# One kernel, seven edits: half-width first projections, normalising on GpSimd, a later top-k selection, a different split of expert passes, and five shared PSUM banks

## The chip, the cores and the metric

The kernel runs on one core of one Trainium2 chip. The metric is the time of one execution on the device, in microseconds (us). The core has five engines that run their own instruction lists in order and wait for each other by semaphores: TensorE (PE, its weight loads shown apart as PEld), VectorE (DVE), ScalarE (ACT), GpSimd (POOL) and SyncE (SP), which here only issues transfers. Transfers (DMA) run on queues beside the engines.

## The reference

512 tokens of width 1024 go through three layers in float32 and a last norm. Cut to what matters:

```python
# layer 1
h = rms_norm(x);  u, q, k, v, f, g1, g2 = split(h @ w_in)
x += (sigmoid(g1) * s5_branch(u) + sigmoid(g2) * forgetting_attention(q, k, v, f)) @ w_out   # 8 heads of 128
x += peer_ffn(rms_norm(x), w_query, sub_keys, peer_u, peer_v)     # 16384 experts, 8 heads x top 16
# layer 2: "even"
y = rmsnorm(x) @ ev_w_in
o_a = dsa_mixer(...)        # 8 latent heads; an indexer scores all tokens and keeps the top 128 of each row
o_b = diff_mixer(...)       # 4 differential heads: softmax_0 - lambda * softmax_1
x += concat(o_a, o_b) @ ev_w_out;   x += swiglu(rmsnorm(x))
# layer 3: "odd"
y = rmsnorm(x) @ od_w_in
o = nsa_mixer(...)          # 16 heads in 4 groups: compressed, selected and window branches, gated
x += o @ od_w_out;   x += swiglu(rmsnorm(x))
out = rmsnorm(x)
```

## The kernel before

All activations stay on the chip as four tiles of 128 tokens. A float32 product is made of three fp32r matmuls (mm3, lines 331 to 334): each operand is split into a high and a low part, and high x high, high x low and low x high are added in PSUM. Weights come in units of 128 x 1024 through Stream (lines 64 to 82): SP issues the load (L67), ACT copies the high part (L75), and DVE subtracts it for the low part (L81), or, for keys that stand in ADDED, ACT writes the negated high part (L78) and a transfer on POOL's queue adds the raw weights to it (L79). Three units are kept ahead of PE.

The program is written as Python generators and a scheduler orders each engine's list from its own estimate of when each instruction can run; nothing is reordered on the chip. Work that is to fill holes (the selection, output projections) is put in a list bg, and each call of yield_bg(n) takes n steps of it at that place in the program; drain_bg takes what is left.

- norm_T (L310 to L329) norms one token tile after another on DVE (xn, L323), transposes it on PE (L326) and splits it on ACT and DVE (hhi L275, hlo L276). A projection with proj_T (L336) multiplies a weight unit with all 512 tokens at once, so its first matmul needs all four tiles. proj_256 (L370) goes tile by tile, but unit by unit outside that.
- Layer 1's expert layer streams peer_u and peer_v, one unit of 512 KB for each of 128 expert blocks, for three of the four token tiles; the rows of the remaining tile's experts are gathered by POOL (L979) and used by DVE (L988, L996). Of the 128 u passes N_SPILL = 72 go before the v passes, with their results written to memory (at) and read back (a4); the last N_LATE = 8 of these come after the last of the gates. The other 56 stand between v passes.
- The even mixer runs the indexer, then 4 differential heads through pipeline, which computes a head's scores (diff_first, L1508) before the head ahead of it is finished (diff_second, L1534: transposes, products, a sum of squares, rsqrt on DVE, on = L1555, and the transposes of on that PE waits for). selection (L1487) is the background of these heads: 16 rounds of MAX8 (L1493) and MATCH_REPLACE8 (L1494) on three rows of tiles, 96 instructions on DVE in 48 steps and a last step that makes masks of them (L1497). It has to be whole before the 8 latent heads. The differential half of the output projection (out_parts, L1599: four column blocks of three steps) is then the background of the latent heads.
- The odd mixer runs 32 items (16 heads x 2 branches) through pipeline: first (L1856) makes four blocks of scores with 128, 256, 384 and 512 keys, each in a PSUM bank of its own from a pair named sx, masks and reduces them on DVE (L1868) and exponentiates on ACT (L1870); second (L1874) scales the four blocks (DVE L1882 for r = 0 and 2, ACT L1880 for r = 1 and 3), transposes them into banks from a set of three named tx (L1887), splits on ACT and DVE, and multiplies with the values (L1897, L1898).
- normalise (L1321) does the same scaling for layer 1's heads and the latent heads: r = 0, 1, 2 on DVE (L1329), r = 3 on ACT.

## Time and profile before

| | |
|---|---|
| median of 3 runs | 3279.72 us (3277.26 to 3280.32) |
| profiled execution | 3279.84 us, of which the span in the trace is 3278.1 us |
| mean granted TensorE clock | 0.978 |
| busy: PE, DVE, ACT, POOL | 95%, 64%, 46%, 22% of the span |

The profile is of one execution. A time at the left of a row counts from the start of the span. A row of a timeline or of a group ends with the idle time of that engine just before, and what ended it. PE clock 1.00 means 2.4 GHz and 0.50 means 1.2 GHz; a stretch's figure is the mean over it.

### The profile page before, as it was taken

The numbers are of one execution on the slowest core, as the hardware profiler recorded it, in microseconds if no ns is written. First come the engines' busy times: TensorE is split into PE (matmuls) and PEld (weight loads), VectorE is DVE, ScalarE is ACT, GpSimd is POOL, SyncE is SP. The second block draws the span as 40 slices with busy tenths as digits, with TensorE's granted clock in tenths as the row PEclk, the third lists the DMA queues.
The fourth block names the chain that finished last, engine by engine and source line by source line (L and its number), as shares of the span: only waits on it lengthen the run. The fifth ranks groups of instructions, "written<-read, shape, count | busy, mean of one in ns | idle before, by whom it ended". The sixth has DMA issues, their size and how long they took to land.

```text
span 3278.1 us, 46646 instructions
## 1 busy us (share of the span) xinstructions
PE 3128.9 (95%) x17107; PEld 2742.3 (84%) x17107; DVE 2108.7 (64%) x4643; ACT 1519.0 (46%) x2966; POOL 709.5 (22%) x873
## 2 busy tenths in 40 slices
PE   7999999999989999999999986999999998999999
PEld 6998878999988878999998975878888986778887
DVE  6786349999757778887885686643324388743323
ACT  4555233559963333333335664632222378732222
POOL 1561000020015554666662310000000110000000
PEclk9999999999999999999999997999999999999999
DMA  6553232476779998999997641122233210123332
GB/s 177 142 136 115 97 116 84 153 247 243 258 271 342 340 342 300 343 336 324 345 335 205 146 107 42 43 90 97 96 97 124 84 46 10 49 73 98 98 92 83
DMA packets 232758, 551.28 MB, mean 168 GB/s; under 512 B 19785, under 2 KB 113865, under 8 KB 230609
## 3 DMA queue, kind: packets, MB, share of 16 engines
q1 hardware_dynamic: 184432, 349.58, 32.1%
q0 software_dynamic: 43776, 159.40, 15.6%
q10 hardware_dynamic: 4320, 39.32, 3.1%
q8 instruction: 134, 2.20, 0.3%
q14 instruction: 96, 0.78, 0.1%
HBM read 472.60 MB, written 49.82 MB: 159 GB/s over the span
## 4 chain that ended last, share of the span: by engine, by line
PE 81%; DVE 10%; ACT 3%; DMA 3%; issue 2%; POOL 0%; SPq 0%; DVEq 0%; POOLq 0%; ACTq 0%
PE mm L332 21%; PE mm L333 21%; PE mm L334 21%; PE ax L334 2%; PE ax L332 2%; PE ax L333 2%; PE ax L1137 2%; DMA wraw<-in_peer_v_dram 1%; DVE wlo L81 1%; PE tx L1317 1%; PE tx L1887 1%; PE po L1897 1%; DVE xn L323 1%; DVE tl L276 1%; ACT whi L75 1%
## 5 line engine op out<-in xcount | busy, mean ns | idle before, releaser
L75 ACT CAST whi<-wraw 128x1024 fp32r<-128x1024 f32 x525 | 549.2, 1048 | 880.1 <-PE mm L333 325.2
L81 DVE TENSOR_TENSOR wlo<-wraw,whi 128x1024 fp32r<-128x1024 f32 x477 | 600.2, 1258 | 544.0 <-ACT whi L75 537.1
L334 PE MATMUL mm<-hhi,wlo 128*128 128x512 f32 (+1 forms) x1544 | 577.8, 374 | 2.6 <-DVE wlo L81 2.6
L332 PE MATMUL mm<-hhi,whi 128*128 128x512 f32 (+1 forms) x1544 | 577.3, 375 | 0.0
L333 PE MATMUL mm<-hlo,whi 128*128 128x512 f32 (+1 forms) x1544 | 577.2, 374 | 0.0
L332 PE MATMUL mm<-whi,hhi 128*128 128x256 f32 (+1 forms) x1280 | 382.1, 300 | 8.1 <-ACT hhi L275 3.9
L333 PE MATMUL mm<-wlo,hhi 128*128 128x256 f32 (+1 forms) x1280 | 382.4, 299 | 2.0 <-DMA wlo<-wraw 2.0
L334 PE MATMUL mm<-whi,hlo 128*128 128x256 f32 (+1 forms) x1280 | 380.3, 299 | 0.0
L334 PEld LDWEIGHTS mm<-hhi,wlo 128*128 128x128 f32 x1544 | 290.1, 188 | 43.3 <-DVE wlo L81 3.2
L332 PEld LDWEIGHTS mm<-hhi,whi 128*128 128x128 f32 x1544 | 290.4, 188 | 41.4 <-ACT hhi L275 0.7
L333 PEld LDWEIGHTS mm<-hlo,whi 128*128 128x128 f32 x1544 | 290.1, 188 | 40.7 <-DVE hlo L276 0.2
L333 PE MATMUL mm<-wlo,wth 128*128 128x512 f32 x768 | 303.5, 395 | 0.1
L334 PE MATMUL mm<-whi,wtl 128*128 128x512 f32 x768 | 302.5, 394 | 0.0
L979 POOL DMA_INDIRECT rw<-in_peer_rows_dram,idx x128 | 159.9, 1249 | 562.4 <-DVE act L988 339.5
L332 PE MATMUL mm<-whi,wth 128*128 128x512 f32 x768 | 257.6, 397 | 9.4 <-ACT whi L75 9.3
L332 PEld LDWEIGHTS mm<-whi,hhi 128*128 128x128 f32 x1280 | 248.4, 194 | 15.6 <-ACT hhi L275 4.1
L333 PEld LDWEIGHTS mm<-wlo,hhi 128*128 128x128 f32 x1280 | 248.3, 194 | 8.9 <-DMA wlo<-wraw 2.2
L334 PEld LDWEIGHTS mm<-whi,hlo 128*128 128x128 f32 x1280 | 247.2, 194 | 5.9
L1203 ACT CAST wth<-w 128x384 fp32r<-128x384 f32 x128 | 65.7, 514 | 354.9 <-POOL w L1200 209.7
L979 POOL DMA_INDIRECT rw<-in_peer_v_dram,idx x128 | 184.8, 1444 | 113.9 <-DVE acc L996 84.0
L988 DVE CUSTOM_DVE_ANT_0 rw<-rw,hrow 128x1024 f32<-128x1024 f32 x128 | 179.5, 1411 | 9.5 <-DMA rw<-in_peer_rows_dram,idx 9.5
L996 DVE SCALAR_TENSOR_TENSOR acc<-rw,act,acc 128x1024 f32<-128x1024 f32 x127 | 173.8, 1369 | 12.7 <-DMA rw<-in_peer_v_dram,idx 12.0
(567 smaller groups left out, 6111.5 us busy)
## 6 DMA issues: line engine op xcount, KB each, us to landing
wraw<-in_peer_u_dram SPq DMA_DIRECT2D x128, 512.0 KB
wraw<-in_peer_v_dram SPq DMA_DIRECT2D x128, 512.0 KB
wlo<-wraw POOLq DMA_DIRECT2D x48, 512.0 KB
gt<-gst ACTq DMA_DIRECT2D x12, 2048.0 KB
g<-gt SPq DMA_DIRECT2D x32, 768.0 KB
wraw<-in_w_gate_dram SPq DMA_DIRECT2D x44, 512.0 KB
wraw<-in_w_up_dram SPq DMA_DIRECT2D x44, 512.0 KB
wraw<-in_w_down_dram SPq DMA_DIRECT2D x44, 512.0 KB
```

The costliest lines, as they stand in the source:

```text
L75: self.nc.scalar.copy(hi[:, :w], r[:, :w])
L81: self.last = self.nc.vector.tensor_sub(lo[:, :w], r[:, :w], hi[:, :w])
L276: V.tensor_sub(lo, ps, hi)
L323: V.scalar_tensor_tensor(xn, x[:, o], rs, grow[:, o], op0=ALU.mult, op1=ALU.mult)
L332: PE.matmul(ps, ah, bh, start=start, stop=False)
L333: PE.matmul(ps, ah, bl, start=False, stop=False)
L334: PE.matmul(ps, al, bh, start=False, stop=stop)
L979: G.indirect_dma_start(out=rw, out_offset=None, in_=A[("peer_rows", "peer_v")[m]], in_offset=bass.IndirectOffsetOnAxis(ap=idx[:, k:k + 1], ...
L988: V.tensor_tensor_reduce(rw, rw, hrow, 1.0, 0.0, op0=ALU.mult, op1=ALU.add, accum_out=act[:, k:k + 1])
L996: V.scalar_tensor_tensor(acc0, rw, act[:, k:k + 1], acc0, op0=ALU.mult, op1=ALU.add)
L1137: PE.matmul(ps[:, i * P:(i + 1) * P], o2[:, i], og[:, i], start=True, stop=True)
L1203: S.copy(wh, w)
```

## The change

1. **Late passes.** N_SPILL goes from 72 to 76, N_LATE from 8 to 12 and DOTS_C from 28 to 32: twelve u passes, not eight, stand between the last gates and the first v pass, and four fewer between v passes.
2. **Halves.** The first three units of w_u, of w_query and of both SwiGLUs (gate 0, up 0, gate 1) are multiplied with the first 256 tokens and then with the last 256 (proj_T_first). These twelve units and the odd mixer's first two become ADDED. The first projections of the even and odd mixer go token tile by token tile over both of their units (by_tile).
3. **GpSimd normalising.** normalise puts r = 0 and 1 on POOL, r = 2 on DVE, r = 3 on ACT, and the odd mixer's second now calls it.
4. **Later selection.** The background steps at the differential heads' projections go from 2 to 1 and between their stages from 3 to 1. Nothing is drained after the heads; three steps are taken after each of four query projections, and three after each of the first six steps of out_parts, which now come before the latent heads.
5. The latent heads' weights (uk, uv) are loaded on POOL's queue, not SP's.
6. The odd mixer's norm gain is loaded ahead of the first SwiGLU.
7. **Shared banks.** The odd mixer has five banks tx for scores and transposes; the scores of r = 0 and 1 share one; all scores of an item are issued ahead of DVE's reading; transposes come as j = 2, then 1 and 3 in one bank, then 0.

```diff
@@ -28,13 +28,15 @@
 NE = 128
-N_SPILL = 72
-DOTS_C = 28
-N_LATE = 8
+N_SPILL = 76
+DOTS_C = 32
+N_LATE = 12
...
-ADDED = ("w_kq", "w_v", "ev_a", "ev_iq", "ev_qk", "ev_vb", "ev_qn")
+ADDED = ["w_kq", "w_v", "ev_a", "ev_iq", "ev_qk", "ev_vb", "ev_qn"]
+ADDED += [(n, m) for n in ("u", "w_query") for m in range(3)] + [("od_kv", 0, kk) for kk in range(2)]
+ADDED += [k for i in range(2) for k in (("gate", i, 0), ("up", i, 0), ("gate", i, 1))]
@@ -73,7 +75,7 @@
         self.nc.scalar.copy(hi[:, :w], r[:, :w])
-        if self.specs[i][0][0] in ADDED:
+        if self.specs[i][0] in ADDED or self.specs[i][0][0] in ADDED:
@@ -338,6 +340,19 @@
+    def proj_T_first(keys, h):
+        us = [ws.get(k, 2 - i) for i, k in enumerate(keys)]
+        pss = [bank_m() for _ in us]
+        for f in range(2):
+            c = slice(256 * f, 256 * f + 256)
+            for ps, (wh, wl) in zip(pss, us):
+                for k in range(KD):
+                    w = slice(k * P, k * P + P)
+                    mm3(ps[:, c], wh[:, w], wl[:, w], h[0][:, k, c], h[1][:, k, c],
+                        k == 0 and f == 0, k == KD - 1 and f == 1)
+        return pss
@@ -367,10 +382,19 @@
-    def proj_256(key, h, c0, nk=KD, tick=2, k0=0):
+    def proj_256(key, h, c0, nk=KD, tick=2, k0=0, by_tile=False):
 
         pss = [bank_m() for _ in range(2)]
-        for kk in range(k0 // 4, nk // 4):
+        if by_tile:
+            us = [ws.get((key, c0, kk), 1) for kk in range(2)]
+        for q in range(NT if by_tile else 0):
+            o = pss[q // 2][:, 256 * (q % 2):256 * (q % 2) + 256]
+            for k in range(KD):
+                wh, wl = us[k // 4]
+                c = slice(k % 4 * 256, k % 4 * 256 + 256)
+                mm3(o, h[0][:, k, q * P:(q + 1) * P], h[1][:, k, q * P:(q + 1) * P], wh[:, c], wl[:, c],
+                    k == 0 and q % 2 == 0, k == KD - 1 and q % 2 == 1)
+        for kk in range(k0 // 4, 0 if by_tile else nk // 4):
@@ -421,6 +445,10 @@
         if 4 + 2 * layer in phases:
+            if layer == 0 and 5 in phases:
+                state["gain"] = ExitStack()
+                state["grow"] = load_gain(A["norm_mix"][1:2], state["gain"].enter_context(
+                    pool_in(tc, name="gain", bufs=1)))
@@ -532,6 +560,7 @@
         V.tensor_sub(wfl, wf, wfh)
+        psu = K["proj_T_first"]([("u", m) for m in range(3)], h)
@@ -826,7 +855,7 @@
         for m in range(4):
-            ps = proj_T(("u", m), h)
+            ps = psu[m] if m < 3 else proj_T(("u", m), h)
@@ -1026,8 +1055,9 @@
                 SY.dma_start(keys, A["sub_keys"])
+                psq = K["proj_T_first"]([("w_query", m) for m in range(3)], h)
                 for m in range(16):
-                    ps = proj_T(("w_query", m), h)
+                    ps = psq[m] if m < 3 else proj_T(("w_query", m), h)
@@ -1266,11 +1296,12 @@
         al = fp.tile([P, NF, T], F32R, name="al")
+        first = K["proj_T_first"]([("gate", i, 0), ("up", i, 0), ("gate", i, 1)], h)
         for m in range(NF):
-            pg = proj_T(("gate", i, m), h)
+            pg = first.pop(0) if first else proj_T(("gate", i, m), h)
             sg = fp.tile([P, T], F32, tag="sg", bufs=3, name=nm("sg"))
             S.activation(sg, pg, AF.Silu)
-            pu = proj_T(("up", i, m), h)
+            pu = first.pop(0) if first else proj_T(("up", i, m), h)
@@ -1323,7 +1354,9 @@
         W = P * (r + 1)
-        if r == NT - 1:
+        if r < 2:
+            nc.gpsimd.tensor_scalar(Ps[r][:, :W], Ps[r][:, :W], fac[:, r:r + 1], None, op0=ALU.mult)
+        elif r == NT - 1:
@@ -1414,7 +1447,7 @@
         qr = ep.tile([P, NT, 8, 32], F32, name="qr")
-        pss = proj_256("ev_a", h, 0)
+        pss = proj_256("ev_a", h, 0, by_tile=True)
@@ -1557,7 +1590,7 @@
             for hd in range(4):
-                pss = proj_256("ev_qk", h, 256 * hd)
+                pss = proj_256("ev_qk", h, 256 * hd, tick=1)
@@ -1575,17 +1608,18 @@
                 if hd < 2:
-                    pss = proj_256("ev_vb", h, 256 * hd)
+                    pss = proj_256("ev_vb", h, 256 * hd, tick=1)
...
-        pipeline(K, diff_heads(), lambda: yield_bg(3))
-        drain_bg()
+        pipeline(K, diff_heads(), yield_bg)
         for m in range(4):
             qn.append([ep.tile([P, T], F32R, tag="qn", bufs=8, name=nm("qn")) for _ in range(2)])
-            stack_even_odd(K, qn[m], proj_T(("ev_qn", m), h))
+            ps = proj_T(("ev_qn", m), h)
+            yield_bg(3)
+            stack_even_odd(K, qn[m], ps)
@@ -1603,7 +1637,12 @@
-        bg.append(out_parts())
+        parts = out_parts()
+        for _ in range(6):
+            next(parts)
+            yield_bg(3)
+        drain_bg()
+        bg.append(parts)
@@ -1611,7 +1650,7 @@
             raw = lp.tile([P, P], F32, tag=name, bufs=2, name=nm(name))
-            SY.dma_start(raw, src[:, hd * P:(hd + 1) * P])
+            G.dma_start(raw, src[:, hd * P:(hd + 1) * P])
@@ -1682,12 +1721,13 @@
     bg, yield_bg, drain_bg = K["bg"], K["yield_bg"], K["drain_bg"]
-    K["banks"](mm=2, po=1, sx=2, tx=3)
+    K["banks"](mm=2, po=1, tx=5)
...
-        h = K["norm_T"](lambda t: xr[:, t, :], A["norm_mix"][1:2], xp, state["sums"])
+        h = K["norm_T"](lambda t: xr[:, t, :], state["grow"], xp, state["sums"])
+    state["gain"].close()
@@ -1715,7 +1755,7 @@
             crow = [qp.tile([P, NT, 4, 2, 64], F32, name=f"crow{i}") for i in range(2)]
-            pss = proj_256("od_kv", h, 0)
+            pss = proj_256("od_kv", h, 0, by_tile=True)
@@ -1857,13 +1897,18 @@
             Ps = []
+            pss = []
             for r in range(NT):
-                W = P * (r + 1)
-                N = max(W, 256)
-                ps = bank("sx")
+                N = max(P * (r + 1), 256)
+                ps = pss[0][:, 256:] if r == 1 else bank("tx")[:, :N] if r else bank("tx")
+                pss.append(ps)
...
+            for r in range(NT):
+                W = P * (r + 1)
+                ps = pss[r]
@@ -1875,27 +1920,29 @@
             V.tensor_mul(den, den, gt[:, :, 3 * hd + 1 + br])
-            for r in range(NT):
-                if r % 2:
-                    S.activation(Ps[r], Ps[r], AF.Copy, scale=den[:, r:r + 1])
-                else:
-                    V.tensor_scalar(Ps[r], Ps[r], den[:, r:r + 1], None, op0=ALU.mult)
-            for j in (0, 1, NT - 1, 2):
+            normalise(K, Ps, den)
+            ts = {}
+            for js in ((2,), (1, 3), (0,)):
+                ps = bank("tx")
+                o = 0
+                for j in js:
+                    for r in range(j, NT):
+                        PE.transpose(ps[:, o:o + P], Ps[r][:, j * P:(j + 1) * P], ident)
+                        o += P
+                j = js[0]
                 W = T - P * j
-                ps = bank("tx")
-                for r in range(j, NT):
-                    PE.transpose(ps[:, (r - j) * P:(r - j + 1) * P], Ps[r][:, j * P:(j + 1) * P], ident)
-                if j == NT - 1:
-                    tf = op.tile([P, W], F32, tag="tf", bufs=2, name=nm("tf"))
-                    S.copy(tf, ps[:, :W])
-                    PE.matmul(po[:64, T - W:], vf[:, br, 64 * g:64 * g + 64], tf, start=False, stop=False)
-                    continue
-                th = op.tile([P, W], F32R, tag=f"th{j}", bufs=2, name=nm("th"))
-                tl = op.tile([P, W], F32R, tag=f"tl{j}", bufs=2, name=nm("tl"))
-                split_ps(th, tl, ps[:, :W])
+                ts[j] = [op.tile([P, W], F32R, tag=f"{n}{j}", bufs=2, name=nm(n)) for n in ("th", "tl")]
+                split_ps(*ts[j], ps[:, :W])
+                if len(js) > 1:
+                    tf = op.tile([P, P], F32, tag="tf", bufs=2, name=nm("tf"))
+                    S.copy(tf, ps[:, W:])
+            for j in (2, 1, 0):
                 v = vx[:, j, br, g].rearrange("p a b -> p (a b)")
-                PE.matmul(po[:, T - W:], v, th, start=False, stop=False)
-                PE.matmul(po[:, T - W:], v, tl, start=False, stop=br == 1 and j == 2)
+                PE.matmul(po[:, P * j:], v, ts[j][0], start=False, stop=False)
+                PE.matmul(po[:, P * j:], v, ts[j][1], start=False, stop=br == 1 and j == 0)
+                if j == 1:
+                    PE.matmul(po[:64, T - P:], vf[:, br, 64 * g:64 * g + 64], tf, start=False, stop=False)
```

On DVE, at the end of the differential heads, the selection stands in the list like this before (sel and m belong to the selection, ry and on to the third head, rv and rt to the last):

```order
L1493 MAX m_2622_20134<-sel_17969 128x8
L1493 MAX m_2623_20137<-sel_17970 128x8
L1493 MAX m_2624_20140<-sel_17971 128x8
L1555 TENSOR_TENSOR on_20031<-po_20019,ry_20037 128x512
L1494 MATCH_REPLACE sel_17969<-m_2622_20134,sel_17969 128x256
L1494 MATCH_REPLACE sel_17970<-m_2623_20137,sel_17970 128x384
L1494 MATCH_REPLACE sel_17971<-m_2624_20140,sel_17971 128x512
L1497 TENSOR_SCALAR sel_17969<-sel_17969 128x256
L1497 TENSOR_SCALAR sel_17970<-sel_17970 128x384
L1497 TENSOR_SCALAR sel_17971<-sel_17971 128x512
```

and like this after the change (here ry and rt belong to the last head, whose on is the next row but one):

```order
L1526 MAX m_2639_20573<-sel_18113 128x8
L1527 MATCH_REPLACE sel_18114<-m_2637_20567,sel_18114 128x512
L1527 MATCH_REPLACE sel_18112<-m_2638_20570,sel_18112 128x256
L269 TENSOR_TENSOR rt_20195<-ry_20182 128x4
L1527 MATCH_REPLACE sel_18113<-m_2639_20573,sel_18113 128x384
L1526 MAX m_2640_20576<-sel_18114 128x8
L1530 TENSOR_SCALAR sel_18112<-sel_18112 128x256
L270 SCALAR_TENSOR_TENSOR rt_20195<-rt_20195,rv_20181 128x4
L1530 TENSOR_SCALAR sel_18113<-sel_18113 128x384
L1527 MATCH_REPLACE sel_18114<-m_2640_20576,sel_18114 128x512
L271 SCALAR_TENSOR_TENSOR ry_20182<-rt_20195,ry_20182 128x4
L1530 TENSOR_SCALAR sel_18114<-sel_18114 128x512
```

Before, three MAX8 and three MATCH_REPLACE8 were left when the third head's on was reached. Now the rounds run on between the steps of the last head's rsqrt, and its on stands behind the last of them; 49 selection instructions stand between the third head's on and the last one's.

On PE, at the start of the first SwiGLU (ax are transposes of the norm's tiles xn, mm the gate and up products), this is the order before:

```order
L326 MATMUL ax_21738<-ident,xn_21736 128x128 x4
L326 MATMUL ax_21747<-ident,xn_21745 128x128 x4
L326 MATMUL ax_21762<-ident,xn_21760 128x128 x4
L326 MATMUL ax_21771<-ident,xn_21769 128x128 x4
L332 MATMUL mm_21796<-hhi_21680,whi_21599 128x512
L332 MATMUL mm_21829<-hhi_21680,whi_21784 128x512
L332 MATMUL mm_21863<-hhi_21680,whi_21788 128x512
L333 MATMUL mm_21796<-hlo_21681,whi_21599 128x512
L334 MATMUL mm_21796<-hhi_21680,wlo_21600 128x512
```

and this after:

```order
L328 MATMUL ax_21879<-ident,xn_21877 128x128 x4
L328 MATMUL ax_21894<-ident,xn_21892 128x128 x4
L334 MATMUL mm_21954<-hhi_21836,whi_21749 128x256
L334 MATMUL mm_21955<-hhi_21836,whi_21940 128x256
L334 MATMUL mm_21956<-hhi_21836,whi_21945 128x256
L328 MATMUL ax_21903<-ident,xn_21901 128x128 x4
L335 MATMUL mm_21954<-hlo_21837,whi_21749 128x256
L336 MATMUL mm_21954<-hhi_21836,wlo_21750 128x256
L334 MATMUL mm_21954<-hhi_21836,whi_21749 128x256
L335 MATMUL mm_21954<-hlo_21837,whi_21749 128x256
L336 MATMUL mm_21954<-hhi_21836,wlo_21750 128x256
```

The products, each now half as wide, start after two and a half tiles, between the transposes of the third; 29 of them stand ahead of the transposes of the fourth tile.

On SP's queue, between the last gates and the first peer_v unit (g and a are read back gates and u results, xr is the residual, four transfers of 512 KB), this was the order:

```order
L67 DMA wraw_10938<-in_peer_u_dram 128x1024
L1193 DMA g_10923<-gt 128x12x128
L1193 DMA a_1410_10919<-at 128x1536
L1193 DMA g_10925<-gt 128x12x128
L447 DMA xr<-x_sc_5467 128x1024 x4
L67 DMA wraw_10976<-in_peer_u_dram 128x1024
L1193 DMA g_11242<-gt 128x12x128
L67 DMA wraw_11014<-in_peer_v_dram 128x1024
L1193 DMA a_1411_10921<-at 128x1536
L1193 DMA g_11378<-gt 128x12x128
```

and it is now:

```order
L69 DMA wraw_11094<-in_peer_u_dram 128x1024
L475 DMA xr<-x_sc_5543 128x1024 x4
L1223 DMA g_11534<-gt 128x12x128
L69 DMA wraw_11132<-in_peer_u_dram 128x1024
L69 DMA wraw_11170<-in_peer_u_dram 128x1024
L1223 DMA a_1413_11077<-at 128x1536
L1223 DMA g_11670<-gt 128x12x128
L69 DMA wraw_11203<-in_peer_u_dram 128x1024
L69 DMA wraw_11236<-in_peer_u_dram 128x1024
L69 DMA wraw_11268<-in_peer_u_dram 128x1024
L1223 DMA g_11806<-gt 128x12x128
L69 DMA wraw_11300<-in_peer_v_dram 128x1024
```

Five units of peer_u now stand between the residual and the first unit of peer_v, where there was one.

## Rows read from the trace of the kernel before

**Rows 1.** The page, part 1: busy time of each engine.

```profile
PE 3128.9 (95%) x17107; PEld 2742.3 (84%) x17107; DVE 2108.7 (64%) x4643; ACT 1519.0 (46%) x2966; POOL 709.5 (22%) x873
```

**Rows 2.** Stretches: length, busy PE PEld DVE ACT POOL, PE clock, DMA share, GB/s.

```profile
0.00:24.00 24.00, 8.87 (x34) 6.61 (x35) 15.39 (x30) 14.61 (x34) 4.57 (x20) 1.00 0.70 242
...
464.00:485.00 21.00, 15.91 (x80) 13.49 (x79) 15.16 (x29) 9.48 (x27) 0.23 (x1) 0.92 0.51 183
...
950.00:985.00 35.00, 27.89 (x148) 26.60 (x147) 12.90 (x12) 11.49 (x18) 8.73 (x8) 0.90 1.01 354
...
1760.00:1790.00 30.00, 25.12 (x177) 23.75 (x176) 15.32 (x32) 19.63 (x36) 4.38 (x6) 0.89 0.69 183
...
1948.00:2014.00 66.00, 24.63 (x118) 20.03 (x118) 46.74 (x153) 27.34 (x85) 2.41 (x4) 0.64 0.13 44
...
2014.00:2106.00 92.00, 84.91 (x549) 74.98 (x547) 65.51 (x175) 59.18 (x149) 3.13 (x6) 0.98 0.12 38
...
2127.00:2145.00 18.00, 12.93 (x64) 10.67 (x63) 14.10 (x27) 8.40 (x18) 0.00 (x0) 0.81 0.18 58
...
2495.00:2525.00 30.00, 24.14 (x146) 22.16 (x145) 17.03 (x31) 11.85 (x24) 2.73 (x9) 0.83 0.55 188
...
2640.00:2874.00 234.00, 217.43 (x1325) 174.28 (x1324) 188.79 (x559) 185.99 (x497) 11.71 (x14) 0.95 0.11 35
...
2820.00:2840.00 20.00, 18.65 (x102) 13.22 (x102) 17.87 (x68) 19.90 (x60) 0.00 (x0) 1.00 0.00 1
...
2895.00:2912.00 17.00, 11.93 (x61) 9.90 (x60) 14.15 (x27) 8.38 (x19) 0.00 (x0) 0.80 0.19 62
```

**Rows 3.** PE's timeline before the first SwiGLU: start, duration, instruction, idle before.

```profile
2127.03 0.39 PE L332 MATMUL mm<-whi,hhi 128*128 128x512 f32 x1
2127.26 0.39 PE L333 MATMUL mm<-wlo,hhi 128*128 128x512 f32 x1
...
2135.89 1.94 PE L326 MATMUL ax<-ident,xn 128*128 128x128 f32 x8 [4.82 <-DVE xn L323]
...
2139.84 1.02 PE L332 MATMUL mm<-hhi,whi 128*128 128x512 f32 x3
```

**Rows 4.** PE's timeline in a projection of 256 columns.

```profile
1800.29 0.28 PE L333 MATMUL mm<-wlo,hhi 128*128 128x256 f32 x1
1800.41 0.28 PE L334 MATMUL mm<-whi,hlo 128*128 128x256 f32 x1
```

**Rows 5.** DVE's groups by line: weight subtraction.

```profile
L81 DVE TENSOR_TENSOR wlo<-wraw,whi 128x1024 fp32r<-128x1024 f32 x477 | 600.2, 1258 | 544.0 <-ACT whi L75 537.1
```

**Rows 6.** DVE's groups by line: top-k selection (busy us, mean ns of one).

```profile
L1493 DVE MAX8 m<-sel 128x8 f32<-128x256 f32 (+2 forms) x48 | 24.8, 550 | 0.2
...
L1494 DVE MATCH_REPLACE8 sel<-m,sel 128x256 f32<-128x256 f32 (+2 forms) x48 | 25.9, 543 | 0.0
```

**Rows 7.** PE's timeline at the end of the differential heads.

```profile
1965.43 1.09 PE L1317 MATMUL tx<-ident,on 128*128 128x128 f32 x4 [13.32 <-DVE on L1555]
...
1992.46 1.08 PE L1317 MATMUL tx<-ident,on 128*128 128x128 f32 x4 [12.68 <-DVE on L1555]
...
2003.28 0.94 PE L1317 MATMUL tx<-ident,on 128*128 128x128 f32 x4 [4.50 <-DVE on L1555]
...
2013.44 0.80 PE L1659 MATMUL mm<-qn,uk 128*128 128x512 f32 x1 [7.26 <-ACT uk L1617]
```

**Rows 8.** ACT's groups by line and shape: normalising in the last layer.

```profile
L1880 ACT ACTIVATE pd<-pd,den 128x256 f32<-128x256 f32 x32 | 16.2, 505 | 1.8 <-DVE den L1877 1.7
```

**Rows 9.** POOL's groups by line and shape: rope.

```profile
L1295 POOL TENSOR_TENSOR rb<-rx,s 128x256 f32<-128x256 f32 x56 | 48.2, 908 | 141.2 <-ACT rx L1292 129.7 <-DVE krow L1789 4.5 <-DVE qrow L1809 2.9
```

**Rows 10.** DVE's timeline: normalising in layer 1, then in the even mixer.

```profile
201.82 1.82 DVE L1329 TENSOR_SCALAR prow<-prow,den 128x128 f32<-128x128 f32 x3
...
2027.84 0.88 DVE L1329 TENSOR_SCALAR pd<-pd,den 128x128 f32<-128x128 f32 x3
```

**Rows 11.** POOL's timeline beside the first of these.

```profile
202.07 0.61 POOL L756 TENSOR_TENSOR st<-st,c 128x256 f32<-128x256 f32 x1
```

4 lines of the change are left out of this document (2 added, 2 removed).

## The prediction

> **What bounds the kernel now.** The first view is the page's busy time: PE is busy 95% of the span [rows 1], so most of the time is matmul work that this change does not remove, and what can be won lies in the other 5%, about 149 us, and in stretches at half clock. The second view cuts the span at PE's idle times [rows 2]. A reader is to compare, row by row, the length, PE's busy time and PE's clock. PE is short of work at the start (8.87 us of 24), at the norm ahead of w_query (464 to 485: 5.1 us idle), at the start of the v passes (950 to 985: 7.1 idle, with the DMA engines full at 354 GB/s), at the even norm (1760: 4.9), the two SwiGLU norms (2127 and 2895: 5.1 each) and the odd norm (2495: 5.9). By far the worst stretch is 1948 to 2014, the end of the differential heads: 24.63 us busy of 66 and a mean clock of 0.64. Each pause is paid twice, since the clock in these rows is below 1 (0.80 to 0.92 at the norms). In the odd heads (2640 to 2874) PE is listed as busy for 217 us of 234, but in 2820 to 2840 ACT is busy 19.90 of 20 us and DVE 17.87: there ACT sets the pace, and PE's busy time is pipelined waiting. The timelines then say what PE waits for: at a norm, for xn of DVE [rows 3]; in the bad stretch, for the heads' on, of which DVE writes each behind selection work, 13.32, 12.68 and 4.50 us, and at the end 7.26 us for uk [rows 7].
>
> **Halves (norms).** Before the first SwiGLU, PE waits 4.82 us between the second and third tile and starts to multiply at 2139.84 [rows 3]. In the new order products stand behind two and a half tiles. PE's list is in order, so it still waits for the third tile's xn, but DVE gets there sooner: two of the weight subtractions of 1.26 us [rows 5] that stand between the tiles' xn are gone from DVE, 2.5 us. Then 29 half products run before the fourth tile's transposes, where PE now has gaps and slow clock. What can be won at most is the idle 5.1 us and the clock's share, 18 x 0.19 = 3.4 us [rows 2], so 8.5; nothing is the other bound, if the low parts, which now take one more ACT pass and a transfer on POOL's queue, come late. ACT is busy 8.4 of these 18 us and hides the pass. I take 5 for this SwiGLU and 5 for the last one, whose row is the same to 0.2 us. By the same reading: w_query idle 5.1 plus 1.7 of clock, where DVE is busy 15 of 21 us on other things, 3; the kernel's start, where PE's loss is 15.1 us but mostly the load of x and the norm of two tiles, 4; the even norm, token tile by token tile, idle 4.9 plus 3.3, 4; the odd norm, which gets that and a gain loaded in advance, idle 5.9 plus 5.1, 6. The bounds are nothing and the sums named.
>
> The price: 12 units of 24 products become two each, 288 more. Products of 512 columns start 0.23 us apart [rows 3] and those of 256 columns 0.12 [rows 4], so a pair costs 0.24: some 0.01 x 288, between 1 and 3 us. I take 2.
>
> **GpSimd normalising.** In layer 1 and the latent heads DVE is not what ends the waits that the views show; I take 1 us for layer 1. In the odd heads ACT loses 32 instructions of 505 ns, 16.2 us [rows 8]. They count only where ACT is the bound. ACT is busy 186 of 234 us in the phase, so 0.79 x 16.2 = 13 if what it gives is proportional; at most 16.2. DVE is next, at 17.87 of 20 in the full stretch, and sheds a block of 128 columns too. GpSimd has no such instruction in the trace. From above, its nearest row is 908 ns for 256 columns with two tensor inputs [rows 9], so 1.4 us at most for both blocks, if the narrow one takes half; from below, DVE's own three blocks in 0.88 us [rows 10], about 0.5 for two. GpSimd is busy 11.71 of these 234 us, so 32 x 1.4 = 45 us fit. What counts is whether its delay is hidden. The transposes of j = 2 need only r = 2 and 3 and come first, and the next item's scores lie ahead, so I hide it. One price is visible: the same three DVE instructions take 0.88 us in the even mixer but 1.82 in layer 1 [rows 10], where GpSimd is running tensor work beside them [rows 11]. That contention would stretch DVE's remaining 384-column block by up to its own length, 0.4 us per item, and bring DVE back to where it was. So DVE stays just under ACT, and I take 11 of the 13.
>
> The Trainium skill has a rule against this edit: the GPSIMD Engine Reference, section 4.1, tells to put elementwise work on VectorE, with GpSimd about half as fast for two inputs and nearly equal for one, and section 8 adds that it shares SBUF interfaces with VectorE. The 1.82 against 0.88 us agree with the second; no row shows the first for one input. By that rule alone the odd heads would give nothing, and the sum would be 3251.
>
> **Shared banks.** Scores of r = 0 and 1 in one bank and five common banks let PE run further ahead. As ACT is the bound, I add nothing; a rotation that makes scores wait for an older transpose could cost a little, which stands in the odd heads' bounds (0 to 18).
>
> **Later selection.** The 96 instructions take 24.8 + 25.9 = 50.7 us of DVE [rows 6], before and after. Before, nearly all of them lie ahead of the third head's on, and PE waits behind them. In the new list 49 stand between the third head's on and the last one's, 49/96 x 50.7 = 26 us. So the second and third head end earlier (the waits of 13.32 and 12.68 us shrink), and the last one's on ends about when it does now: the third at some 1975 instead of 1992, then 26 us and the rsqrt steps between them, 2003 to 2010 against 2003.28 [rows 7]. PE has 27 products of the moved output columns to fill this wait; 69 wait behind on for 69 x 0.12 = 8.3 us at full clock, 14.5 at half. They cover the 7.26 us for uk, whose load is also no longer behind the residual on SP. So the latent heads start at 2016 to 2024 instead of 2013.44, with 96 x 0.12 = 11.5 us less to do as background in their 92 us, of which PE is busy 84.91. I take 9 of these. Together between 12 won and 12 lost; I take 0.
>
> **Late passes.** Of the loss at 950 to 985 (7.1 idle and 3.5 of clock), the cause is a full queue: gates, u results and 2 MB of residual ahead of the first peer_v unit. Five u passes, not one, now stand between, so that unit has time; but the queue is as full, and the wait may come at a u unit. The work is the same number of passes. I take 3, between 0 and 8, and as much as 3 lost if the four more read-backs hold up the v passes. The remaining edits cost nothing by themselves: uk on POOL's queue lies where GpSimd is busy 3 of 92 us.
>
> **Sum.** 4 + 1 + 3 + 3 + 4 + 0 + 5 + 6 + 11 + 5 = 42, less 2, is 40: from the profiled 3279.84 us (span 3278.1, 1.7 around it) to 3240. The median of the runs shown, 3279.72, is the same to 0.1.
>
> **Rivals.** (a) The selection's new tail decides: the last on comes late because each rsqrt step waits behind three selection instructions, and PE, with nothing left, waits for it at half clock. Plus 12 instead of 0: 3252. For it: the list; against: DVE's work before it shrinks by as much. (b) The odd heads give nothing, by contention or because the transposes of j = 0 and 1 wait for GpSimd: 3251. (c) The halves don't act, because PE's list still waits for the third tile's xn and the low parts come late: the norms give 9 of 27, 3258. (d) The even mixer gains: if half of the 41 us that PE is idle in 1948 to 2014 and some of its clock come back, 30 more: 3210. (e) Slower than before: GpSimd's two blocks stand in the chain of every odd item. At 1.4 us, with 0.9 of contention by [rows 10], less the 0.5 that ACT saves, an item grows by 1.8, 32 x 1.8 = 58, and 3240 + 11 + 58 = 3309. It decides from 0.9 us per item on, where it eats the other 29.
>
> **How the numbers follow.** Forecast 0.46; (a) 0.18, (b) 0.13, (c) 0.09, (d) 0.07, (e) 0.07. The likeliest is 3240. Its own terms leave about 15 us either way; to keep (a), (b) and (c) in and most of (d) and (e) out, the range is 3218 to 3264. About 0.2%, 6.5 us, is what a measurement of this kernel can tell from no change; only (e), and a little of (c), reach to it. Faster 0.91, within 0.2% 0.03, slower 0.06.
>
> **What would show it.** In the changed profile: no gap of 4.8 us at the norms, half-width products between the tiles' transposes, and a clock above 0.9 there; ACT at its limit in the odd heads and the phase near 223 us, not 234; GpSimd's blocks below 1 us each; a PE wait of 20 us or more ahead of the last on, and none for uk; the first peer_v unit without a wait of 7 us. The prediction is wrong if the odd phase is not shorter, if DVE's 384-column blocks take twice as long as before and DVE becomes the bound, or if the last on comes after 2015.

## The result, and the profile after

The changed kernel takes 3316.14 us (median of 5 runs, 3311.76 to 3322.57), against 3279.72 us before on the same chip: ratio 1.0116, 95% interval 1.0105 to 1.0127. Forecast were 3240 us, so it went the other way: 36 us slower instead of 40 faster. The profiled execution has a span of 3314.3 us, 36.2 more than before. The page's busy times of the changed kernel:

```profile
PE 3140.5 (95%) x17395; PEld 2763.2 (83%) x17395; DVE 2099.7 (63%) x4565; ACT 1522.0 (46%) x2948; POOL 803.0 (24%) x999
```

PE is busy for 11.6 us more than before and ACT for 3 [rows 1], GpSimd for 93. Of the 36 us, 24.6 are more idle time of PE, and the 11.6 are in a busy time that also grows where the clock is lower. The stretches of the changed kernel that answer to those of before, in the same columns as [rows 2] (length, busy PE, PEld, DVE, ACT, POOL, PE clock, DMA share, GB/s):

```profile
0.00:24.00 24.00, 10.34 (x42) 8.61 (x43) 11.08 (x25) 15.93 (x35) 4.39 (x14) 1.00 0.76 237
...
464.00:487.00 23.00, 19.96 (x133) 18.53 (x132) 13.89 (x30) 12.38 (x31) 1.96 (x3) 0.93 0.85 252
...
950.00:1000.00 50.00, 36.87 (x203) 36.23 (x203) 15.20 (x14) 14.68 (x23) 9.12 (x8) 0.86 0.81 284
...
1779.00:1806.00 27.00, 22.11 (x168) 21.58 (x167) 13.06 (x27) 15.65 (x28) 4.18 (x6) 0.87 0.66 184
...
1965.00:2042.00 77.00, 33.40 (x197) 30.32 (x197) 60.20 (x193) 24.43 (x77) 6.04 (x12) 0.69 0.11 40
...
2042.00:2152.00 110.00, 100.98 (x557) 83.45 (x557) 69.39 (x171) 69.19 (x173) 21.85 (x31) 0.97 0.15 45
...
2149.00:2167.00 18.00, 15.40 (x121) 14.62 (x121) 12.46 (x25) 10.34 (x22) 1.73 (x2) 1.00 0.57 147
...
2519.00:2545.00 26.00, 20.18 (x132) 18.52 (x132) 14.75 (x26) 9.72 (x18) 6.71 (x13) 0.87 0.58 185
...
2659.00:2912.00 253.00, 220.35 (x1329) 180.44 (x1328) 187.11 (x535) 178.38 (x472) 66.70 (x78) 0.91 0.10 32
...
2840.00:2860.00 20.00, 16.19 (x85) 12.18 (x84) 16.42 (x57) 17.31 (x51) 4.41 (x6) 0.91 0.08 28
...
2934.00:2951.00 17.00, 14.43 (x105) 13.79 (x104) 11.73 (x23) 9.93 (x19) 1.71 (x2) 0.90 0.61 155
```

Read against [rows 2]: the first SwiGLU's norm has become good (2149: 2.6 us idle at full clock, before 5.1 at 0.81), the last one's too (2934: 2.6 at 0.90); at w_query's PE is idle for 3.0 us instead of 5.1, and the even and odd norms (1779, 2519) have gained hardly anything. The stretch of the late passes is worse (950: PE idle for 13.1 us of 50, before 7.1 of 35). And in the odd heads ACT, which was busy for 186 of 234 us, is busy for 178 of 253, and for 17.31 of a 20 us stretch where it was busy for 19.90: it no longer sets the pace.

The clearest account comes from landmarks, the start of the same instruction in both traces (the last one is the end of PE's last matmul). Spans between them in us, from the profiles; the last column is the sum of the prediction's terms for that span (2 us for the halves' price lie outside):

| from, to | before | changed | difference | forecast |
|---|---|---|---|---|
| start, transposes at w_query's norm | 467.5 | 469.4 | +1.9 | -5 |
| to the even norm (w_query, u, late and v passes) | 1296.5 | 1309.3 | +12.8 | -6 |
| to the last indexer score (even norm) | 97.6 | 99.4 | +1.8 | -4 |
| to the first SwiGLU's norm (heads, selection) | 267.4 | 273.4 | +6.0 | 0 |
| to the odd mixer's first key transposes (two norms) | 483.7 | 475.7 | -8.0 | -11 |
| to the last SwiGLU's norm (odd heads) | 284.4 | 308.5 | +24.1 | -11 |
| to the end | 373.1 | 370.9 | -2.2 | -5 |

Two spans make the failure: the odd heads, 35 us off, and the late passes, 19 off.

How far a span of a single profile can be trusted is seen where kernels share a part. Up to w_query's norm, before_own_a4 (below) has the instructions of the kernel before and takes 464.7 us, 2.8 less. The odd heads of the changed form take 308.5, 307.1 and 304.0 us in the three kernels that have them whole, and those of the old form 284.4, 284.4 and 279.8 in three others. Differences of less than some 5 us between two profiles are therefore not certain.

### The profile page after: what moved, and what is told of

Same layout as the page of the kernel before. It is cut to its first block, busy times and chain, and to the rows that moved or that the text cites. A ratio compares the mean times of both kernels' runs of the same rounds, so it can differ in the third digit from the quotient of the medians.

```text
span 3314.3 us, 47383 instructions
## 1 busy us (share of the span) xinstructions
PE 3140.5 (95%) x17395; PEld 2763.2 (83%) x17395; DVE 2099.7 (63%) x4565; ACT 1522.0 (46%) x2948; POOL 803.0 (24%) x999
## 4 chain that ended last, share of the span: by engine, by line
PE 61%; DVE 5%; ACT 2%; DMA 2%; issue 1%; POOL 1%; DVEq 0%; ACTq 0%; POOLq 0%; SPq 0%
PE mm L335 15%; PE mm L334 15%; PE mm L336 15%; PE ax L334 3%; PE ax L336 3%; PE ax L335 3%; PE tx L1931 1%; DMA wraw<-in_peer_v_dram 1%; PE tx L1348 1%; PE po L1942 1%; DVE sel L1527 1%; DMA wlo<-wraw 1%; DVE pd L1913 1%; ACT whi L77 1%; DVE m L1526 0%
## 5 line engine op out<-in xcount | busy, mean ns | idle before, releaser
L334 PE MATMUL mm<-hhi,whi 128*128 128x512 f32 (+2 forms) x1640 | 596.5, 364 | 5.5 <-ACT hhi L277 4.3
L336 PE MATMUL mm<-hhi,wlo 128*128 128x512 f32 (+2 forms) x1640 | 594.9, 363 | 3.4 <-DMA wlo<-wraw 2.1
L335 PE MATMUL mm<-hlo,whi 128*128 128x512 f32 (+2 forms) x1640 | 596.7, 364 | 0.3 <-DVE hlo L278 0.3
L334 PEld LDWEIGHTS mm<-hhi,whi 128*128 128x128 f32 x1640 | 310.1, 189 | 43.6 <-ACT hhi L277 4.9
L336 PEld LDWEIGHTS mm<-hhi,wlo 128*128 128x128 f32 x1640 | 310.0, 189 | 41.3 <-DMA wlo<-wraw 2.4
L335 PEld LDWEIGHTS mm<-hlo,whi 128*128 128x128 f32 x1640 | 310.4, 189 | 36.6 <-DVE hlo L278 0.5
L335 PEld LDWEIGHTS mm<-wlo,hhi 128*128 128x128 f32 x1280 | 250.0, 195 | 10.2 <-DMA wlo<-wraw 4.3
L81 POOL DMA_DIRECT2D wlo<-wraw x62 | 54.9, 885 | 754.7 <-ACT wlo L80 727.5
```

The lines of the kernel that those rows point to most:

```text
L81: self.nc.gpsimd.dma_start(lo[:, :w], r[:, :w], accum_op=ALU.add)
L334: PE.matmul(ps, ah, bh, start=start, stop=False)
L335: PE.matmul(ps, ah, bl, start=False, stop=False)
L336: PE.matmul(ps, al, bh, start=False, stop=stop)
```

## The experiments

Theories. For the odd heads: A, GpSimd's blocks stand in the chain of each item (the prediction's rival e); B, the shared banks and the new order, which the prediction priced at nothing. For the late passes: the number of passes, the traffic, or a buffer.

**The odd mixer's scaling undone** (odd_scale_back). In second, `normalise(K, Ps, den)` is replaced by the old lines:

```diff
-            normalise(K, Ps, den)
+            for r in range(NT):
+                if r % 2:
+                    S.activation(Ps[r], Ps[r], AF.Copy, scale=den[:, r:r + 1])
+                else:
+                    V.tensor_scalar(Ps[r], Ps[r], den[:, r:r + 1], None, op0=ALU.mult)
```

> The changed kernel with the odd mixer's scaling back on VectorE (r = 0, 2) and ScalarE (r = 1, 3); banks and order stay as changed. Theory A, GpSimd's 1.79 us for two blocks stand in the chain of each item: the odd heads lose the 18 us that they grew by, the whole is about 3298, and with the freer banks perhaps a few us less. Theory B, the five shared banks and the order of transposes cost the time: within 4 us of the changed kernel, 3312 to 3320.

3301.58 us, ratio to before 1.0063 (1.0046 to 1.0081); the odd heads take 299.0 us. That is 9.5 of the 24 us lost there. Theory A holds for a part; 15 us stay without GpSimd's scaling.

**The odd mixer's banks and order undone** (odd_banks_back), GpSimd kept:

```diff
-    K["banks"](mm=2, po=1, tx=5)
+    K["banks"](mm=2, po=1, sx=2, tx=3)
...
-                ps = pss[0][:, 256:] if r == 1 else bank("tx")[:, :N] if r else bank("tx")
+                ps = bank("sx")
...
-            for js in ((2,), (1, 3), (0,)):
+            for j in (0, 1, NT - 1, 2):
```

> The changed kernel with the odd mixer's two score banks, three transpose banks, interleaved scores and old order of transposes; GpSimd still scales r = 0 and 1. Theory A (GpSimd in the chain): no gain, and a loss of some us, since the old order starts with j = 0, which needs GpSimd's blocks first: 3316 to 3340. Theory B (banks and order): about 3298.

3285.80 us, ratio 1.0022 (1.0010 to 1.0033). The odd heads take 276.0 us, 8.4 less than before the change and 32.5 less than in the changed kernel. So B, and more than B promised. In the span ahead of them this kernel takes 477.4 us and the changed one 475.7: there the five banks help a little.

Not all of the 8.4 us are GpSimd's. halves_only (below) has the odd heads of before, without GpSimd, and takes 279.8 us for them, 4.6 less than the kernel before; why is not shown. Against it, the four kernels with the old banks and GpSimd's scaling (276.0, 277.4, 276.2 and 275.8 us) win 2.4 to 4.1. No run undoes the scaling alone under the old banks.

GpSimd's groups in this kernel (partitions x elements, count, busy us and mean ns, idle before and what ended it; 32 of the 40 are in the odd mixer):

```profile
L1358 POOL TENSOR_SCALAR pd<-pd,den 128x256 f32<-128x256 f32 x40 | 37.9, 948 | 0.0
...
L1358 POOL TENSOR_SCALAR pd<-pd,den 128x128 f32<-128x128 f32 x40 | 29.6, 739 | 165.2 <-DVE den L1917 50.7 <-ACT th L277 30.4 <-DVE den L1677 29.4
```

and in the changed kernel:

```profile
L1358 POOL TENSOR_SCALAR pd<-pd,den 128x256 f32<-128x256 f32 x40 | 40.9, 1021 | 0.0
...
L1358 POOL TENSOR_SCALAR pd<-pd,den 128x128 f32<-128x128 f32 x40 | 29.9, 747 | 189.4 <-DVE den L1922 77.3 <-ACT pd L1915 30.6 <-DVE den L1677 29.3
```

The same instructions take nearly the same time, 1.7 to 1.8 us per item. What differs is seen first at PE. The odd heads of the changed kernel, then of the one with the old banks (columns as in [rows 2]):

```profile
2627.20:2935.70 308.50, 275.85 (x1689) 230.77 (x1689) 220.22 (x594) 207.39 (x526) 76.97 (x90) 0.92 0.12 38
...
2629.30:2905.30 276.00, 261.52 (x1653) 215.57 (x1652) 217.00 (x591) 203.96 (x525) 72.96 (x88) 0.98 0.14 43
```

PE is idle for 32.7 us instead of 14.5, at a mean clock of 0.92 instead of 0.98. What it waits for in these stretches (line, us in total, times, longest), in the changed kernel:

```profile
PE po L1978 <- DVE o L1992: 7.4, 6, 1.9
PE po L1978 <- DVE oT L1992: 7.2, 7, 2.5
...
PE tx L1931 <- POOL pd L1358: 1.5, 4, 0.5
```

and with the old banks:

```profile
PE tx L1923 <- POOL pd L1358: 1.6, 3, 0.8
...
PE po L1967 <- DVE o L1981: 1.1, 3, 0.5
...
PE po L1967 <- DVE oT L1981: 0.3, 1, 0.3
```

The largest part is a wait that the prediction does not name. Both kernels have a single bank po for a head's result; the first product of the next head takes it when DVE has read it (L1992, L1981). In the changed kernel PE waits for that 14.6 us in 13 heads, with the old banks 1.4 us. For GpSimd's blocks it waits no longer than with the old banks; but in odd_scale_back the wait for po is 6.3 us, so a part of what GpSimd costs may lie there. In the kernels below that take parts of the new form it is 1.8 us with only the new second stage and 6.0 with only the new first stage. A second bank po was not tried.

ACT shows another part in the splitting of the transposed blocks. With the old banks:

```profile
L277 ACT CAST th<-tx 128x512 fp32r<-128x512 f32 x48 | 28.0, 583 | 17.8 <-PE tx L1923 10.2 <-PE tx L1372 7.6
...
L277 ACT CAST th<-tx 128x384 fp32r<-128x384 f32 x48 | 22.9, 477 | 2.5 <-PE tx L1923 1.9 <-PE tx L1372 0.2
...
L277 ACT CAST th<-tx 128x256 fp32r<-128x256 f32 x48 | 17.7, 368 | 7.4 <-PE tx L1923 5.1 <-PE tx L1372 2.3
```

and in the changed kernel:

```profile
L277 ACT CAST th<-tx 128x512 fp32r<-128x512 f32 x48 | 28.2, 587 | 12.2 <-PE tx L1372 7.6 <-PE tx L1931 4.5
...
L277 ACT CAST th<-tx 128x384 fp32r<-128x384 f32 x48 | 23.0, 478 | 10.6 <-PE tx L1931 10.0 <-PE tx L1372 0.2
...
L277 ACT CAST th<-tx 128x256 fp32r<-128x256 f32 x48 | 17.7, 368 | 14.1 <-PE tx L1931 11.6 <-PE tx L1372 2.0
```

ACT's waits for the transposes of the odd mixer (lines 1923 and 1931) are 17.2 us with the old banks and 26.1 with the new ones, most of them now ahead of the first two splits. The chain of work of the changed kernel inside one item:

```profile
2846.53 0.25 PE po L1943
...
2846.82 1.66 POOL pd L1358 x2
...
2848.52 1.97 PE tx L1931 x8
```

1.66 us of GpSimd, then eight transposes: here GpSimd's two blocks stand one behind the other in the chain. (The view puts GpSimd's start down to a product; by the code it waits for den, which DVE had written at 2846.63.) PE itself stood idle for them for 0.19 us only, so this item alone does not explain the loss.

**Which part of the new form.** Six kernels, with one execution each, take parts of it; all have the read-backs' own buffers (below) and GpSimd's scaling. They are read by the span of the odd heads alone.

odd_new_second keeps the old first stage and banks (sx=2, tx=3) and takes only the new second stage.

> The changed kernel with own buffers for the read-backs (it starts the odd mixer some 16 us earlier, so the odd heads are read as a phase of their own). In the odd mixer only the second stage is the new one: GpSimd scales r = 0 and 1, transposes come as 2, then 1 and 3 in one bank, then 0, values last; scores have two banks of their own, interleaved with VectorE's reading, and transposes three. If the second stage's order is what stretches the items (the joint bank of 1 and 3 waits for GpSimd's r = 1 and ScalarE's r = 3 together, and no product starts before all splits), the odd heads stay 15 to 20 us longer than before. If the scores' sharing does it, they become about 10 us shorter than before.

odd_new_first takes only the five banks, the pair and the joint issue of scores; the second stage is the old one.

> As the run before, but only the first stage and the banks are the new ones (r = 0 and 1 share a score bank, all scores ahead of VectorE's reading, five banks for scores and transposes); the second stage has its old order 0, 1, 3, 2 with four transposes' banks, and GpSimd scales r = 0 and 1. If the shared banks and the scores issued together are the cause (a transposes' bank is taken by scores of the next item), the odd heads are 15 to 20 us longer than before; if the second stage is, about 10 us shorter.

odd_five_banks takes only `K["banks"](mm=2, po=1, tx=5)` and `ps = bank("tx")` in the old first stage; odd_pair_bank only `ps = pair[:, 256:] if r == 1 else bank("sx")`.

> With own buffers for the read-backs. In the odd mixer, of the new form only the five banks are taken, given in turn to scores and transposes; each block of scores has a bank of its own, VectorE's reading stands between the scores, the second stage is the old one with GpSimd scaling. From the kdup transposes to the last norm before took 284 us, the changed kernel 308, the old banks with GpSimd 277, the new first stage 305. If the turn-taking over one set of banks stretches it (a block of scores takes the bank that transposes of the item ahead, which wait for GpSimd, still hold or are to get), some 300 or more here. If it is the pair or the joint issue of scores, 277 to 282.

> As the run before, but with two banks for scores and three for transposes, and only the pairing taken: scores of r = 0 and 1 in one bank, VectorE's reading between the scores, old second stage with GpSimd. If the pair is the cause (the bank comes free only when both blocks are read), 295 to 305 for the odd heads; if the five banks are, 275 to 280.

odd_five_pair joins those two; odd_joint_own issues the paired scores jointly into three banks of their own (sx=3, tx=2).

> Own read-back buffers; in the odd mixer five banks in turn and the pair of r = 0 and 1, but VectorE's reading stands between the scores; old second stage, GpSimd scaling. If the joint issue of scores is what adds the rest (305 against 287 for the five banks alone), the odd heads take 286 to 291. If five banks and the pair together do it, 300 to 306.

> Own read-back buffers; scores paired and issued jointly into three banks of their own, transposes in two banks, old second stage, GpSimd scaling. If the joint issue by itself stretches the items (three banks must be free before the first score, and all are taken before any is read), 295 or more. If it does so only where scores and transposes take turns in one set, 277 to 287, the upper end for transposes that have two banks instead of three.

| odd mixer, with GpSimd's scaling | odd heads, us |
|---|---|
| old banks, old order (a4_and_banks) | 277.4 |
| only the pair in one bank | 279.0 |
| only the new second stage | 282.7 |
| only five banks in turn | 286.9 |
| five banks and pair | 294.1 |
| pair and joint issue, own banks (two for transposes) | 298.9 |
| five banks, pair, joint issue | 304.7 |
| all of the new form (late_own_a4) | 307.1 |

Three of these runs fell between the readings that their expectations set against each other (282.7, 286.9 and 294.1), so no single part is the cause. The five banks cost 10 us, the pair 7 on top of them (2 alone), the joint issue 11 on top of both; the second stage costs 5 alone and 2 on top. The prices of 2 and 5 are within what two profiles can differ by. With banks of its own the joint issue costs 20 (298.9 against 279.0), in line with the expectation's reading that it stretches the items by itself; but the transposes have one bank less in that kernel, and the run does not part the two.

**The late split undone** (late_back): N_SPILL, DOTS_C and N_LATE at 72, 28 and 8.

> The changed kernel with 72 passes ahead, 8 late and 28 gather steps, as before. If the 12 late passes cost the time between 956 and 1120 us, the stall of 12.88 us at 975 falls back to about 7 and the drift of 8 us up to 1120 goes: 3316 less 15 to 17 is about 3300. If that loss comes from another edit (the halves of w_query, through the gathered tile's later start), it stays: 3313 to 3319.

3292.96 us, 1.0037 (1.0023 to 1.0051). The span to the even norm is 1292.1 us, 17.2 less than in the changed kernel: the split costs it, as long as the read-backs share buffers with the late results, and not the halves.

**Own buffers for the read-backs** (late_own_a4): the 12 late passes write their results to tiles with the tag a4, of which there are two, and the read-backs used the same two. This edit gives the read-backs two of their own (not three, as its expectation says).

```diff
-                    d[q] = vp.tile(shape, F32, tag=tag, bufs=2 if tag == "a4" else 3, name=nm(tag))
+                    d[q] = vp.tile(shape, F32, tag=tag, bufs=2 if tag == "a4r" else 3, name=nm(tag))
...
-            ahead(s4, e // 4, N_SPILL // 4, lambda q: at[q], "a4", [P, 4, TD])
+            ahead(s4, e // 4, N_SPILL // 4, lambda q: at[q], "a4r", [P, 4, TD])
```

> The changed kernel, all 12 late passes kept, but with the read-backs of the u results in three buffers of their own instead of the two that the late passes write to. If the stall is the buffer (ScalarE's write of the second late group waits for GpSimd's product, which waits for a read-back, which waits for the first group's store), the wait at 975 goes wholly, 12 us, and part of the drift with it: 3298 to 3305. If it is the traffic of the queue, the wait moves to a wraw and the time stays at 3312 to 3318.

3297.35 us, 1.0055 (1.0039 to 1.0072), and the span to the even norm is again 1292.1 us, now with all twelve passes. Twelve late passes with their own buffers are thus worth nothing against eight. The timelines show the chain. ACT of the changed kernel (as is a late pass's result, at its place in memory):

```profile
969.93 0.48 ACT L1204 ACTIVATE as<-ax 128x384 f32<-128x384 f32 x1
...
971.10 0.33 ACTq L1206 DMA_DIRECT2D at<-as  x1
...
987.31 0.87 ACT L1204 ACTIVATE as<-ax 128x384 f32<-128x384 f32 x2 [2.02 <-POOL w L1230]
```

GpSimd:

```profile
982.72 4.56 POOL L1230 TENSOR_TENSOR w<-a,g 128x384 f32<-128x384 f32 x4 [13.79 <-DMA a<-at]
```

and PE:

```profile
987.85 0.69 PE L334 MATMUL ax<-hhi,whi 128*128 128x384 f32 x1 [12.88 <-ACT as L1204]
```

The first late group is stored at 971.10; its buffer is then filled by a read-back, for which GpSimd's four products wait until 982.72; only when they have read it, at 987.3, may ACT write the second group's first result, and PE waits 12.88 us for the PSUM bank that ACT has not emptied. With own buffers ACT goes on (same columns):

```profile
968.06 0.33 ACTq L1206 DMA_DIRECT2D at<-as  x1
...
972.56 0.48 ACT L1204 ACTIVATE as<-ax 128x384 f32<-128x384 f32 x1
...
975.86 0.49 ACT L1204 ACTIVATE as<-ax 128x384 f32<-128x384 f32 x1 [2.81 <-PE ax L336]
```

**The same buffers in the kernel before** (before_own_a4), to see whether its 7.1 us wait was the same.

> The kernel before with only the read-backs in buffers of their own. If the wait of 7.1 us at 973 was the same chain of the shared buffers, it goes and the time falls by 4 to 7 us, 3273 to 3276. If it was the full queue ahead of the first peer_v unit, as I read it, no change: 3277 to 3281.

3282.18 us, 1.0005 (0.9995 to 1.0015): no gain. In the kernel before ACT is held up too, from the store at 967.69 to 983.43, where with own buffers it goes on at 968.15. But with only two results waiting in the two PSUM banks of ax, PE's next work is the first v pass, and what it waits for is peer_v's weights:

```profile
983.43 0.86 ACT L1174 ACTIVATE as<-ax 128x384 f32<-128x384 f32 x2
...
979.94 2.93 PE L332 MATMUL mm<-whi,wth 128*128 128x512 f32 x6 [7.11 <-ACT whi L75]
```

With own buffers this wait comes later:

```profile
993.38 2.93 PE L332 MATMUL mm<-whi,wth 128*128 128x512 f32 x6 [5.27 <-ACT whi L75]
```

Over 940 to 1200 us PE's waits for these weights are 8.5 us before and 9.6 with own buffers. That fits the prediction's reading of this stretch, a full queue ahead of peer_v: weights that come late, not the buffers, set its length.

**Both mended** (a4_and_banks).

> The changed kernel with both mended: own buffers for the read-backs, and the odd mixer's old banks and order with GpSimd scaling. If the two causes are separate, the gains add: 3316 less 18 less 30 is 3268, faster than before by 0.3%. If they are one (a shift of something else), the time is that of the better one, 3286.

3268.29 us, 0.9965 (0.9951 to 0.9979): the two add, and the kernel is faster than before.

**And the selection where it was** (a4_banks_sel): the old steps, drain and output columns.

> The same, and the selection where it was before (two and three steps, drained ahead of the query projections, output columns all behind the latent heads). If the later selection costs the 6 us that the two traces show between the indexer and the first SwiGLU, 6 us below the run before, 3262. If it only moves the wait, the same within 3.

3261.96 us, 0.9951 (0.9934 to 0.9968). The ranges of this kernel's and the last one's times overlap, so the difference of 6.3 us is not certain from the times alone. From the last indexer score to the first SwiGLU's norm this kernel takes 262.6 us and the one with the later selection 268.9; all kernels here with the later selection take 268.9 to 273.4 and all with the old one 262.6 to 267.9. PE's waits for on in the changed kernel:

```profile
1974.98 1.08 PE L1348 MATMUL tx<-ident,on 128*128 128x128 f32 x4 [9.78 <-DVE on L1588]
...
1999.64 1.09 PE L1348 MATMUL tx<-ident,on 128*128 128x128 f32 x4 [11.90 <-DVE on L1588]
...
2027.34 1.08 PE L1348 MATMUL tx<-ident,on 128*128 128x128 f32 x4 [20.16 <-DVE on L1588]
```

Before they were 13.32, 12.68 and 4.50 us [rows 7]. The second and third head's have shrunk by 4 in all and the last has grown by 16. Times from the last indexer score on show the same: the transposes of the third head's on start after 121.5 us (before 130.8), those of the last head's after 149.2 (before 141.6), and the latent heads' first product after 163.6 (before 151.8). That this kernel beats the one before by 4.8 us in this span goes with uk, which edit 5 loads on POOL's queue: PE waits 1.26 us for it here and 7.26 before [rows 7].

**Layer 1 as before, too** (a4_banks_sel_l1): w_u in whole units, scaling of layer 1's heads on DVE.

> The kernel with own read-back buffers, the odd mixer's old banks with GpSimd, and the old selection, and now in layer 1 also whole u projections and scaling on VectorE as before. The traces show layer 1 some 2 to 3 us later at w_query than before with the halves and GpSimd there. If GpSimd's scaling holds up the state-space chain on GpSimd and the halves of u save nothing, layer 1 is back at 467.5 and the time 3 us lower, 3259; if the halves of u are worth the forecast 4, it is 2 to 4 us higher, 3265.

3257.41 us, 0.9922 (0.9905 to 0.9938), the fastest kernel of this study, with 467.8 us to w_query's norm against 470.3. Its interval and that of the run before overlap slightly, so the 4.5 us between the medians are not certain, nor are the 2.5 us in the span of single profiles.

**The halves alone** (halves_only): the kernel before with proj_T_first, by_tile, the keys in ADDED and the early gain.

> The kernel before with only the halves, the projections by token tile, the keys in ADDED and the early norm gain. My forecast for these was 27 less 2, 3255. By the phases of the changed kernel (both SwiGLU norms and the odd norm together about 9, w_query 1, the even norm none, the start none), 3268 to 3272.

3283.07 us, 1.0007 (0.9994 to 1.0020): no gain, where 3268 to 3272 was expected. In its profile, of an execution of 3277.04 us, the two spans with the SwiGLU norms and the odd norm are 3.7 and 3.6 us shorter than before, but the span to w_query's norm is 478.1 us, 10.6 longer. PE's waits in layer 1 there, which the profile of before shows smaller or not at all:

```profile
181.86 0.49 PE L841 MATMUL tx<-Sr,CL 128*128 128x128 f32 x2 [2.50 <-POOL Sr L831]
...
184.01 1.12 PE L1348 MATMUL tx<-ident,qn 128*128 128x128 f32 x4 [1.54 <-DVE kql L281]
...
210.69 0.66 PE L1348 MATMUL tx<-ident,qn 128*128 128x128 f32 x4 [1.36 <-ACT kt L763]
```

They are for the state-space part on GpSimd and the heads' operands on DVE and ACT, and make up some 3.5 of the 10.6 us. That the earlier u products shift that part's order is likely, and was not tried further; the changed kernel, with the same halves of u and with GpSimd's scaling, takes 469.4 us there, so the loss hangs on more than the halves.

## Why the prediction was wrong

- **Shared banks: the step that failed.** "As ACT is the bound, I add nothing." The edit of banks and order costs 32.5 us in the odd heads against the same kernel with the old banks (some 30 in the whole time): 24 lost where 11 were to be won. The step took PE's running ahead for a gain only. What the runs show in its place is that ACT is no longer the bound and PE stands idle for 18 us more, 13 of them for the one bank po, at a lower clock. The parts cost 10 (five banks in turn), 7 (pair) and 11 us (joint issue) together. Why in detail is argued, not shown: scores and transposes that take banks in one fixed turn wait for each other's readers, and scores issued together need all their banks before DVE has anything to read. The clause kept in the bounds ("a rotation that makes scores wait for an older transpose could cost a little") came near the mechanism, but the bounds of 0 to 18 hold no loss.
- **GpSimd's scaling: the term was too large.** Under the old banks it is worth 2.4 to 4.1 us against halves_only, at most 8.4 against the kernel before, forecast 11. Its blocks are longer than what the prediction called the most for both: 1.02 and 0.75 us, 1.77 together, where that was 1.4; the narrow one takes three quarters of the wide one, not half. The price of contention, 0.4 us per item, was read from one case of 1.82 against 0.88 us. DVE's 384-column block took 414 ns in the odd mixer before; on average it takes 433 in the changed kernel and 469 with the old banks, so 0.02 to 0.06 us per item. Before, changed, and with the old banks:

```profile
L1882 DVE TENSOR_SCALAR pd<-pd,den 128x384 f32<-128x384 f32 x32 | 13.2, 414 | 0.0
...
L1362 DVE TENSOR_SCALAR pd<-pd,den 128x384 f32<-128x384 f32 x40 | 17.3, 433 | 1.2
...
L1362 DVE TENSOR_SCALAR pd<-pd,den 128x384 f32<-128x384 f32 x40 | 18.7, 469 | 0.9
```

  Rival (e), GpSimd in the chain, came true for a part and only together with the new banks: undoing GpSimd there gives 9.5 us against the changed kernel, 5 against the fastest of the three that have the new form whole.
- **Late passes: the wait was looked for in the wrong place.** "the queue is as full, and the wait may come at a u unit" has the price 3 won, or at most 3 lost; 13 were lost over the span, by a buffer that late results and read-backs share. The sharing is as old as the kernel; four more late passes make PE need the bank that ACT cannot empty meanwhile. With own buffers the span is 4.4 us shorter than before, near the 6 forecast for w_query and the late passes, but it is as short with eight late passes: the late passes' 3 did not come.
- **Selection: rival (a), at half its price.** The prediction had the latent heads start 3 to 11 us later and 9 us less to do behind that, together 0. They started 11.8 us later, with 5.8 saved behind: measured +6.0. The step that failed is the third head's on, expected some 17 us earlier and come 9 earlier; the selection work behind it then took as long as forecast, and PE waits 20.16 us for the last on. That PE waits no longer for uk came true.
- **Halves: mechanism right at the SwiGLU norms, size two thirds at most, and hardly anything elsewhere.** The spans with the two SwiGLU norms and the odd norm give 10.2 us together, forecast 16; halves_only gives 7.3, so some of the 10.2 may be the five banks' ahead of the odd heads. At the even norm and the start there is nothing, forecast 4 and 4; at w_query's PE is idle for 2.1 us less, forecast 3. The first products do start earlier (at the first SwiGLU the clock stays at 1.00). That in layer 1 PE is not what the next 100 us wait for is likely, not shown.
- The sum treated the edits as independent. Two of them, GpSimd and the banks, were not: a gain of some us alone, a loss of 5 to 9.5 in company. Nor were the late passes and the buffers that they share. Even the fastest kernel of this study wins some 26 us (ratio 0.9922) of the 40, with the later selection and layer 1's edits undone, and with a gain from uk that the prediction had inside a term of 0.

## What to carry to other kernels

An edit that only moves waiting, a bank shared, a buffer given out in turn, a list reordered, has no price in any busy time; before pricing it at nothing, write down for each buffer who must have read it before the next writer may go, and follow that chain once through the new order. When one engine has just been relieved, look at what was hidden behind it. And a bundle should be undone part by part: here two edits that cost 30 and 19 us hid a gain of 11.

## What was not expected of the hardware

GpSimd's scaling of 128 columns by one factor per row took 0.75 us and of 256 columns 1.02 us in the changed kernel, with a single tensor input, where DVE took 0.33 us for 128 columns (odd mixer before) and 0.35 us for 256 (latent heads before): two to three times as long. The Trainium skill (GPSIMD Engine Reference, section 4.1) calls one-input work on GpSimd nearly equal to VectorE's; at these sizes the runs do not show that. Under the old banks it was still some gain, as GpSimd had the time.
